# Where the SBUF tiles of a two-layer backbone kernel begin, modulo 512 bytes

## The chip, the core and the metric

The kernel runs on one core of a Trainium2 chip. The metric is the device time of one execution in microseconds (us). SBUF is the on-chip memory that the engines read. A tile of 128 partitions begins at the same byte in each partition, and this text calls that byte modulo 512 the tile's **place**. TensorE is PE in the profile, and PEld is its weight load. VectorE is DVE, ScalarE is ACT, GpSimd is POOL, and SyncE (SP) issues the DMAs.

## What is computed

A layer of the first kind (a gated depthwise convolution of 31 taps beside windowed attention) is followed by one of the second kind (a gated convolution of 3 taps), and by a final RMS norm. Tokens: 512, with a context of 256; width 1024, inner width 2048. Most of the arithmetic is in four matrix products:

```python
h = xn @ w_in                                  # layer one: 1024 -> 4608 columns
x = x + gt * ((concat(a, att) * silu(gate)) @ ev_w_out)
h = xn @ od_w_in                               # layer two: 1024 -> 8192 columns: bg, cg, u, z
x = x + gt * ((bg * conv3(cg * u) * silu(z)) @ od_w_out)
return rms_norm(x, final_g)
```

## The kernel before

Both operands of a product are split in two halves of type float32r, a rounded `h` and the rest `l`, and each product is three matmuls:

```python
def mm3(out, wh, wl, xh, xl, start, stop):
    T.matmul(out, lhsT=wh, rhs=xh, start=start, stop=False)
    T.matmul(out, lhsT=wh, rhs=xl, start=False, stop=False)
    T.matmul(out, lhsT=wl, rhs=xh, start=False, stop=stop)
```

The tile given as `lhsT` is stationary: a LDWEIGHTS loads 128 columns of it (512 bytes of each partition) ahead of its matmul. The tile given as `rhs` is moving: the matmul streams it, 512 columns (2048 bytes) in most. Each matmul has a LDWEIGHTS of its own, also where the stationary tile is the one before.

`proj` makes a projection: 8 steps over the width of 1024, so 24 matmuls into one PSUM bank, with the weight tile stationary and the activations moving. Layer two runs `mixer(j)` for j = 0 to 15, and each calls `in_proj(j)`: four projections (`pcg`, `pu`, `pbg`, `pz`), 96 matmuls. For j = 0 they are cut into halves of 256 columns. For j = 1 to 15 they are whole: 15 x 96 = 1440 matmuls of 512 columns. After that the outputs `f` are made, in two halves of the model's width, with the weights `wf` moving and the activations `z1h`, `z1l` stationary; a weight block `wf_0` to `wf_7` holds two of the 16 steps. In layer one, the projections `pq`, `pk`, `ag`, `av`, `pg` are mixed among the matmuls of attention (`s`, `pt`, `po`), `pgc` comes after them, and then come 8 projections `pya` with weights `woa` (192 matmuls) on the gated attention.

All operations are recorded and put into an order by a planner that uses costs written in the code; it knows nothing of addresses. So each operation is issued from one line, L481. SBUF comes from one pool. A tile has a tag, and the pool gives a tag one block of buffers when the tag is first used; block follows on block in that order. Tags of small or odd size (`cols` with 1664 bytes, columns of 4 to 128 bytes) are first used between the large ones, so the large ones begin at different places. In the built program they are:

| tag | holds, where TensorE reads it | place before | place after |
|---|---|---|---|
| `wh`, `wl` | weight halves: stationary in projections, moving in `f` | 256 | 128 |
| `xn` | activations of layer one (moving); `z` of the convolution; `z1` for j < 8 (stationary in `f`) | 256 | 128 |
| `q` | queries (stationary in `s`); `z1` for j = 8 to 11 | 256 | 128 |
| `D` | keys; first weights `ws`; gated attention `z8` to `z15` (moving in `pya`); `yh`, `yl` (moving in layer two); last three `wf` blocks of the second half | 384 | 128 |
| `p` | attention weights; weights of `in_proj(0)`; `z1` for j = 15 | 384 | 128 |
| `vv` | values (stationary in `po`); weights of `in_proj(0)` | 384 | 128 |
| `th`, `tl` | transposed attention weights (moving in `po`); `z1` for j = 12 and 13 | 128 | 128 |
| `tmp`, `sg`, `wsv`, `rx`, `pacc`, `wr` | work tiles; `sg` holds `z1` for j = 14 | 256, 256, 256, 128, 0, 320 | 128 |
| `A`, `B`, `rope`, `ad` | tokens, `x1`, modulation weights | 384 or 128 | the same |
| `ident`, `ones` | identity of the transposes, row of ones | 320, 256 | the same |

Slices of a tile that TensorE takes begin 512 or 1024 bytes further on, so they have the tile's place.

Of the kernel before, what the change touches and what calls it, by code (L numbers as in the profile page):

```python
# [11 lines left out]
F32 = mybir.dt.float32  # L12
# [7 lines left out]
P = 128  # L20
D = 1024
# [463 lines left out]
def backbone_kernel(ctx, tc, x_d, ctx_d, xT_d, c_d, cT_d, cols_d, ada0_d, ada1_d, adas_d, ws_d, wi0_d, woa_d, woc_d, wi1_d, wo1_d,  # L485
# [11 lines left out]
    pool = ctx.enter_context(tc.tile_pool(name="sb", bufs=1))  # L497
    ps = ctx.enter_context(tc.tile_pool(name="ps", bufs=1, space=PSUM))

    def new(shape, dt, tag, name, bufs, space=pool):  # L500
        t = LTile(space, shape, dt, tag, name, bufs, space is ps)
        return View(t, [], 0, shape[0], t.ix, dt)


    phases = Phases(lambda k: tc.tile_pool(name=f"ps{k}", bufs=1, space=PSUM))
# [5 lines left out]
    def bank(tag, name):  # L511
        if tag == "c":
            return phased(2, (P, 512), "c", name, 3)
        return new((P, 512), F32, tag, name, {"b": 4, "cv": 1}[tag], ps)
# [3 lines left out]
    def unit(tag, name, dt=F32, shape=(P, 512)):  # L518
        return new(tuple(shape), dt, tag, name, TAGS[tag])


    dm = new((P, 1), F32, "dm", "dm", 1)
    V.memset(dm, 1.0)
    A_.activation(dm, dm, AF.Silu)
# [329 lines left out]
    vv = new((P, NB, NKV, P), F32R, "vv", "vv", 1)  # L854
# [199 lines left out]
    with plan.after(turned[-1]), plan.stream("ada", ADA_BIAS):  # L1054
        silc = new((P, D), F32, "rope", "silc", 1)
        SP.dma_start(out=silc, in_=c_d[0:1, :].to_broadcast([P, D]))
        for n in range(2):
            th = unit("tmp", f"silt{n}")
# [369 lines left out]
```

## Time and profile before

| | us |
|---|---|
| median of 3 runs (lowest, highest) | 1018.12 (1016.85, 1019.17) |
| the profiled execution: its own time | 1019.33 |
| its span, first to last instruction | 1017.5 |
| PE busy in the span | 982.0 |
| DVE, ACT, POOL busy in the span | 609.6, 488.5, 412.5 |

Matmuls overlap each other, so the length that the profile gives for one (0.39 us or so for 512 columns) is not what it costs. In a stretch without gaps the cost of one is the distance from its start to the next one's start: the starts of the first and the last row of a run of matmuls, divided by their number. The text calls this the spacing.

### The profile page before, as it was taken

The numbers are of one execution on the slowest core, as the hardware profiler recorded it, in microseconds if no ns is written. First come the engines' busy times: TensorE is split into PE (matmuls) and PEld (weight loads), VectorE is DVE, ScalarE is ACT, GpSimd is POOL, SyncE is SP. The second block draws the span as 40 slices with busy tenths as digits, with TensorE's granted clock in tenths as the row PEclk, the third lists the DMA queues.
The fourth block names the chain that finished last, engine by engine and source line by source line (L and its number), as shares of the span: only waits on it lengthen the run. The fifth ranks groups of instructions, "written<-read, shape, count | busy, mean of one in ns | idle before, by whom it ended". The sixth has DMA issues, their size and how long they took to land.

```text
span 1017.5 us, 13484 instructions
## 1 busy us (share of the span) xinstructions
PE 982.0 (97%) x4996; PEld 806.0 (79%) x4996; DVE 609.6 (60%) x982; ACT 488.5 (48%) x923; POOL 412.5 (41%) x368
## 2 busy tenths in 40 slices
PE   8989999999999997799998999999999999999997
PEld 5888777778787786588898988888888888888886
DVE  4735878978888888856217576444444444542343
ACT  6637779676797754344326332232223223222232
POOL 5616887666979867878867000000000000000011
PEclk9989999999999999799999999999999999999999
DMA  8632111012122335243254245223222322322322
GB/s 323 228 120 82 65 43 39 26 61 95 51 84 105 118 108 188 81 168 104 82 173 140 83 156 175 104 83 104 84 102 83 104 96 92 104 83 84 102 83 83
DMA packets 31750, 109.11 MB, mean 107 GB/s; under 512 B 3650, under 2 KB 3778, under 8 KB 31684
## 3 DMA queue, kind: packets, MB, share of 16 engines
q1 hardware_dynamic: 31684, 108.25, 31.0%
q8 instruction: 39, 0.64, 0.3%
q14 instruction: 27, 0.22, 0.1%
HBM read 106.14 MB, written 2.10 MB: 106 GB/s over the span
## 4 chain that ended last, share of the span: by engine, by line
PE 76%; DVE 9%; DMA 5%; ACT 4%; POOL 3%; issue 2%; SPq 0%; POOLq 0%; DVEq 0%; ACTq 0%
PE pbg L481 9%; PE pz L481 9%; PE pcg L481 9%; PE pu L481 9%; PE f L481 8%; PE pya L481 5%; PE s L481 3%; DVE cv L481 3%; PE po L481 3%; PE pt L481 3%; PE ag L481 3%; PE pq L481 3%; PE av L481 3%; PE pg L481 2%; PE pgc L481 2%
## 5 line engine op out<-in xcount | busy, mean ns | idle before, releaser
L481 POOL TENSOR_TENSOR x1t<-x1t,fg 128x512 f32<-128x512 f32 x4 | 6.8, 1738 | 402.1 <-ACT fy L481 402.1
L481 DVE SCALAR_TENSOR_TENSOR cv<-u,cols,cv 128x512 f32<-128x512 f32 x180 | 135.5, 753 | 12.2 <-ACT cv L481 8.2
L481 POOL TENSOR_TENSOR cp<-cp,pr 128x512 f32<-128x512 f32 x60 | 78.9, 1315 | 3.5 <-ACT pr L481 1.6
L481 DVE TENSOR_TENSOR tl<-pt,th 128x512 fp32r<-128x512 f32 x72 | 48.1, 689 | 22.6 <-ACT th L481 21.4
L481 PE MATMUL pt<-ident,p 128*128 128x128 f32 x288 | 49.5, 277 | 3.4 <-ACT p L481 2.8
L481 ACT ACTIVATE th<-pt 128x512 fp32r<-128x512 f32 x72 | 41.1, 595 | 20.3 <-PE pt L481 19.4
L481 ACT ACTIVATE p<-s,nm 128x512 f32<-128x512 f32 (+1 forms) x64 | 46.9, 739 | 7.3 <-DVE nm L481 6.9
L481 PEld LDWEIGHTS pt<-ident,p 128*128 128x128 f32 x288 | 35.8, 140 | 17.2 <-ACT p L481 10.1
L481 DVE TENSOR_REDUCE s<-s 128x2 f32<-128x1024 f32 (+1 forms) x32 | 43.5, 1360 | 4.1 <-PE s L481 3.7
L481 ACT ACTIVATE pr<-u,cols 128x512 f32<-128x512 f32 x60 | 41.4, 718 | 5.6 <-POOL cp L481 4.1
L481 PE MATMUL po<-th,vv 128*128 128x512 f32 x72 | 31.2, 433 | 0.6 <-ACT th L481 0.5
L481 PE MATMUL po<-tl,vv 128*128 128x512 f32 x72 | 31.0, 431 | 0.2 <-DVE tl L481 0.2
L481 DVE TENSOR_TENSOR ya<-ya,sz 128x512 f32<-128x512 f32 x16 | 11.1, 691 | 32.4 <-ACT sz L481 32.3
L481 DVE SCALAR_TENSOR_TENSOR ac<-ac,silc 128x1024 f32<-128x1024 f32 x6 | 9.6, 1599 | 31.9 <-DMA ac<-in_ada_dram 31.9
L481 ACT ACTIVATE sz<-pz 128x512 f32<-128x512 f32 x16 | 9.6, 597 | 36.0 <-PE pz L481 36.0
L481 DVE SCALAR_TENSOR_TENSOR ya<-cu,cols,ya 128x512 f32<-128x512 f32 x32 | 24.1, 752 | 1.1
L481 PEld LDWEIGHTS pmod<-ccol,adas 128*128 128x128 f32 x128 | 19.0, 226 | 2.8 <-DMA adas<-in_adas_dram 2.2
L481 DVE TENSOR_TENSOR ya<-pbg,ya 128x512 f32<-128x512 f32 x16 | 11.1, 692 | 14.5 <-PE pbg L481 14.4
L481 PE MATMUL pmod<-ccol,adas 128*128 128x2 f32 x128 | 18.7, 267 | 0.9 <-DMA adas<-in_adas_dram 0.6
L481 ACT ACTIVATE tp<-tp,mab 128x512 f32<-128x512 f32 (+1 forms) x16 | 10.2, 640 | 19.1 <-PE tp L481 13.5
L481 PEld LDWEIGHTS po<-th,vv 128*128 128x128 f32 x72 | 13.5, 188 | 6.6 <-ACT th L481 5.7
L481 PEld LDWEIGHTS po<-tl,vv 128*128 128x128 f32 x72 | 13.7, 190 | 5.1 <-DVE tl L481 3.3
(1671 smaller groups left out, 3460.7 us busy)
## 6 DMA issues: line engine op xcount, KB each, us to landing
wicg<-in_wi_dram SPq DMA_DIRECT2D x16, 512.0 KB, 3.3
wiu<-in_wi_dram SPq DMA_DIRECT2D x16, 512.0 KB, 3.3
wibg<-in_wi_dram SPq DMA_DIRECT2D x16, 512.0 KB, 3.3
wiz<-in_wi_dram SPq DMA_DIRECT2D x16, 512.0 KB, 3.4
wf<-in_wo_dram SPq DMA_DIRECT2D x16, 512.0 KB, 3.3
adas<-in_adas_dram SPq DMA_DIRECT2D x8, 512.0 KB, 4.0
ada<-in_ada_dram SPq DMA_DIRECT2D x8, 512.0 KB, 5.0
wb<-in_wi_dram SPq DMA_DIRECT2D x8, 512.0 KB, 3.4
```

Source lines behind the costliest of these rows:

```text
L481: op.a = op.fn(*a, **k)
```

## The change

Before any tile of the kernel is used, one tile of each of 15 tags is taken from the pool and not used. All 15 sizes are multiples of 512 bytes, so their blocks follow on each other at one place, and the tags of odd size come behind them. The row of instructions of each engine, and the semaphores that each instruction waits for, are the same as before; only addresses differ. The places that result are in the last column of the table above.

```diff
+    for tag, n, bufs in (("wr", 1024, 3), ("D", 512, 16), ("xn", 512, 16), ("q", 512, 8), ("wh", 512, 4), ("wl", 512, 4),
+                         ("tmp", 512, 4), ("p", 640, 8), ("vv", 3072, 1), ("th", 512, 2), ("tl", 512, 2), ("wsv", 256, 8),
+                         ("sg", 512, 2), ("rx", 512, 1), ("pacc", 512, 1)):
+        pool.tile([P, n], F32, tag=tag, name=f"place_{tag}", bufs=bufs)
+
+
     phases = Phases(lambda k: tc.tile_pool(name=f"ps{k}", bufs=1, space=PSUM))
```

## Rows read from the trace of the kernel before

**Rows 1.** The page: busy time, share of the span and instructions of each engine.

```profile
PE 982.0 (97%) x4996; PEld 806.0 (79%) x4996; DVE 609.6 (60%) x982; ACT 488.5 (48%) x923; POOL 412.5 (41%) x368
```

**Rows 2.** Busy time by stretch: attention, `pya`, layer two's projections, first half of `f`.

```profile
core 0: us, PE busy (x) PEld busy (x) DVE busy (x) ACT busy (x) POOL busy (x), PEclk, DMA share, GB/s
78.00:386.00 308.00, 303.15 (x1625) 238.91 (x1625) 252.06 (x387) 232.03 (x447) 231.37 (x208) 1.00 0.23 77
...
451.00:500.00 49.00, 48.57 (x224) 39.23 (x224) 26.93 (x39) 21.30 (x36) 40.20 (x31) 1.00 0.29 97
...
584.00:920.00 336.00, 336.00 (x1442) 270.27 (x1442) 164.02 (x271) 100.00 (x166) 0.00 (x0) 1.00 0.31 105
920.00:966.00 46.00, 46.00 (x210) 37.82 (x209) 15.56 (x23) 13.75 (x24) 1.81 (x2) 1.00 0.27 92
```

**Rows 3.** The chain that ended last, in order of time: start us, us, what.

```profile
584.10 5.60 PE pcg L481 x24
...
936.27 69.97 PE f L481 x334
```

**Rows 4.** Timeline of PE: first matmul of `in_proj(1)`, first of `f` (start us, us).

```profile
583.94 0.40 PE L481 MATMUL pcg<-yh,wicg1h 128*128 128x512 f32 x1
...
919.94 0.39 PE L481 MATMUL f<-wf_0h,z1h 128*128 128x512 f32 x1
```

**Rows 5.** Timeline of PE: projection `av` 5 of layer one, first, and the 24 behind.

```profile
233.78 0.39 PE L481 MATMUL av<-xh,wa5h 128*128 128x512 f32 x1
...
239.22 0.39 PE L481 MATMUL av<-xl,wa4h 128*128 128x512 f32 x1
```

**Rows 6.** Timeline of PE: first matmuls of `pya` 4 and of `pya` 5.

```profile
476.43 0.40 PE L481 MATMUL pya<-z8h,woa4h 128*128 128x512 f32 x1
...
482.03 0.40 PE L481 MATMUL pya<-z8h,woa5h 128*128 128x512 f32 x1
```

**Rows 7.** Timeline of PE, first half of `f`: first matmuls with `wf` 5, 6, 7.

```profile
949.30 0.39 PE L481 MATMUL f<-wf_5h,z1h 128*128 128x512 f32 x1
...
954.75 0.40 PE L481 MATMUL f<-wf_6h,z1h 128*128 128x512 f32 x1
...
960.34 0.39 PE L481 MATMUL f<-wf_7h,z1h 128*128 128x512 f32 x1
```

**Rows 8.** Timeline of PE, second half of `f`, third block of tokens.

```profile
1001.90 0.39 PE L481 MATMUL f<-wf_5h,z1h 128*128 128x512 f32 x1
...
1003.29 0.39 PE L481 MATMUL f<-wf_6h,z1h 128*128 128x512 f32 x1
...
1004.66 0.40 PE L481 MATMUL f<-wf_7h,z1h 128*128 128x512 f32 x1
...
1005.37 0.39 PE L481 MATMUL f<-wf_7h,z1h 128*128 128x512 f32 x1
...
1005.83 0.40 PE L481 MATMUL f<-wf_7h,z1l 128*128 128x512 f32 x1
```

**Rows 9.** Timeline of PE, second half of `f`: behind a run of 256 columns.

```profile
971.41 0.40 PE L481 MATMUL f<-wf_1h,z1h 128*128 128x512 f32 x1
...
972.80 0.39 PE L481 MATMUL f<-wf_1h,z1h 128*128 128x512 f32 x1
```

**Rows 10.** Timeline of PE: matmuls of 256 columns, `in_proj(0)` and `f`.

```profile
574.77 0.28 PE L481 MATMUL pbg<-yl,w 128*128 128x256 f32 x1
...
575.97 0.28 PE L481 MATMUL pu<-yh,wiu0l 128*128 128x256 f32 x1
...
1006.06 0.28 PE L481 MATMUL f<-wf_5h,z1h 128*128 128x256 f32 x1
...
1006.30 0.28 PE L481 MATMUL f<-wf_5h,z1l 128*128 128x256 f32 x1
```

**Rows 11.** Groups of DVE in 695.94 to 718.35 us: count, busy us, mean ns.

```profile
L481 DVE TENSOR_TENSOR wiz6l<-wiz,wiz6h 128x512 fp32r<-128x512 f32 x2 | 1.4, 694 | 4.2 <-ACT wiz6h L481 4.2
...
L481 DVE TENSOR_TENSOR z1l<-ya,z1h 128x512 fp32r<-128x512 f32 x1 | 0.7, 693 | 0.1
```

## The prediction

> **What bounds the kernel now.** I read the page first, then busy time by stretch, then the chain of waits, and last the timeline of PE row by row. The page shows PE busy for 982.0 of 1017.5 us [rows 1], and the stretches show where that is a bound [rows 2]: in layer two's projections PE is busy for all of 336.00 us, with DVE at 164.02, ACT at 100.00, POOL at nothing and the DMA engines at 0.31. In `pya` it is 48.57 of 49, in the first half of `f` 46.00 of 46. The chain that ended last goes through PE there without a break, projection after projection of 24 matmuls in 5.60 us, then 334 matmuls of `f` in 69.97 us [rows 3]. So from 584 us to about 1006 us only the spacing of the matmuls counts, and a shorter spacing shortens the kernel one to one. Attention is less pure: PE 303.15 of 308, DVE 252.06, ACT 232.03 [rows 2].
>
> **Two spacings.** The timeline is to be read for starts, not lengths. From the first matmul of `in_proj(1)` to the first of `f` there are 1440 matmuls of 512 columns in 919.94 - 583.94 = 336.00 us: 233.3 ns each [rows 4]. The projection `av` 5 has the same shape, the same code and the same count, and takes 239.22 - 233.78 = 5.44 us: 226.7 ns each [rows 5]. `pya` 4 takes 482.03 - 476.43 = 5.60 us: 233.3 ns [rows 6]. [...]
>
> What differs is the pair of places. `av` streams `xn` (256) over `wh`, `wl` (256). `pya` and layer two stream `D` (384) over the same tags (256). That alone could still be the stage, so I looked for a stage in which the pair changes and nothing else does. That is `f`, with `wf` moving and `z1` stationary:
> - first half, `wf` 5 over `q`: 256 and 256, 24 matmuls in 954.75 - 949.30 = 5.45 us, 227.1 ns [rows 7];
> - first half, `wf` 6 over `th`, `tl`: 256 and 128, 960.34 - 954.75 = 5.59 us, 232.9 ns [rows 7];
> - second half, `wf` 5 (now in `D`) over `q`: 384 and 256, 6 matmuls in 1003.29 - 1001.90 = 1.39 us, 231.7 ns [rows 8];
> - second half, `wf` 6 (in `D`) over `th`, `tl`: 384 and 128, 1004.66 - 1003.29 = 1.37 us with the odd pair at its end, 228 ns [rows 8].
>
> Each stationary tag and each moving tag stands once in a fast pair and once in a slow one. So it isn't the tag, the engine that wrote it, or the stage: where the two places differ by 0 or 256 the spacing is about 227 ns, where they differ by 128 it is about 233. I call the first pairs even and the second odd. An odd pair costs 233.3 - 226.7 = 6.6 ns more.
>
> **The change part by part.** No instruction and no wait is added, removed or moved, so the change costs nothing in itself. The 15 unused tiles take no time. What it does is to make every pair among the 15 tags even (128 and 128). Counted in the program's order of matmuls, of 512 columns each:
> - Layer two, j = 1 to 15: 1440 odd pairs become even: 1440 x 6.6 = 9.5 us [rows 4, 5]. All of it is on the chain [rows 3].
> - `pya`: 192 odd pairs (24 x 8) become even: (5.60 - 5.44) x 8 = 1.3 us [rows 5, 6]. On the path, PE is busy throughout there [rows 2].
> - `f`: 36 odd pairs in the first half and 27 in the second: 63 x 6 = 0.4 us [rows 7, 8].
> - Attention, 78 to 386 us: 170 matmuls of 512 columns go from odd to even, at most 170 x 6.6 = 1.1 us. Against that, 127 short matmuls (transposes by `ident`, which stays at 320, and the masks) are now followed by a stationary tile at 128 in place of 256, an odd difference. The trace has no clean run of such a pair. With nothing or 6.6 ns each as bounds the cost is 0 to 0.8 us. A gain on either side can also be lost in waits for ACT and DVE. I take 0.3 us of gain, bounds -0.8 and +1.1.
> - Matmuls of 256 columns: the pairs of `in_proj(0)` are even already (384 and 384), 10 in 1.20 us, 120 ns [rows 10]. An odd pair (`wf` 5 in `D` over `q`) takes 2 in 0.24 us, the same, so I take nothing for them [rows 10].
> - First 78 us: about 150 odd pairs become even, at most 150 x 6.6 = 1.0 us. Most are of 256 columns, and the weights are still being loaded there, so I take nothing.
> - DVE, ACT and POOL read and write at other places too. DVE's subtraction of two halves takes 694 ns with its tiles at 256, 320 and 256, and 693 ns with all three at 256 [rows 11]. I take nothing, for ACT and POOL too.
>
> Sum: 9.5 + 1.3 + 0.4 + 0.3 = 11.5 us. Against its own time the profiled execution would go from 1019.33 to 1007.8. It lies 1.2 us over the median of 1018.12, so as a median I expect **1006.6 us**, 0.989 of before.
>
> **The one price that isn't in the trace.** No pair of before is 128 and 128. The nearest rows are 384 and 128, and 256 and 256, both at 227 ns; they show that neither the 256 nor the difference of 256 matters. The other bound are the rows of 384 and 384 at the end of `f` (`wf` 7 over `p`): two matmuls in 1005.83 - 1005.37 = 0.46 us, 230 ns [rows 8]. I take 226.7, because those two stand between odd pairs, and even pairs need some matmuls to settle: behind a run of 256 columns, 6 even pairs of 256 and 256 take 972.80 - 971.41 = 1.39 us, 231.7 ns [rows 9], and then drop to 227. Layer two has no such disturbance between its 1440 matmuls.
>
> [...] The trace has 226.7 and 233.3 ns for the same matmul with its tiles at other places [rows 5, 6]. [...]
>
> **The rivals.**
> - *No change, 1018.1.* The two reads don't meet, and 6.6 ns is a property of the stage (what ACT and DVE do beside it, which banks are written). For it: most odd pairs lie in two stages. Against it: within `f`, the spacing changes at the very matmul at which the pair changes, in both directions [rows 7, 8].
> - *The place itself matters, 1010 to 1017.* If 128 and 128 settles between 227 and 230 ns as 384 and 384 may [rows 8], the 1690 odd pairs on the path (1440 + 192 + 63, less a few at seams) gain less and some 1185 pairs that are even already (attention, `pgc`, `f`) lose. At 228.5: 1690 x 4.8 - 1185 x 1.8 = 6.0 us of gain, 1012.1. At 230: 1.7 us, 1016.4.
> - *Slower, 1026.* Two reads that begin at one place might always meet. If 128 and 128 costs what an odd pair costs, 233.3 ns, layer two and `pya` gain nothing and the 1185 even pairs lose 6.6 ns each: 7.8 us more, 1025.9. The change turns slower where the spacing of 128 and 128 passes 230.6 ns, since 1690 x (233.3 - s) = 1185 x (s - 226.7) there. Against it: 256 and 256 is also one place, and it is the fastest pair that the trace has [rows 5, 7].
> - *Another bound takes over.* In 336 us DVE works for 164.02 and ACT for 100.00 [rows 2], and 9.5 us less leaves both far off. I give it no chance of its own.
>
> **How the numbers follow.** The forecast (10 to 13 us of gain, so 1005 to 1008.5) has 0.80, a greater gain by way of attention 0.02, the place itself 0.08, no change 0.05, slower 0.05. The runs of before spread over 0.23%, so 0.2% (2 us) is about what can be told from no change. Faster by more than that: 0.80 + 0.02 + 0.06 of the third = 0.88. Within it: 0.02 + 0.05 = 0.07. Slower: 0.05. The range takes in the bounds of attention and the nearer part of the third case: 1004.5 to 1011.
>
> **What would show it.** In the profile after: projections of layer two with 24 matmuls in 5.44 us instead of 5.60, the first matmul of `f` some 11 us earlier and 326.4 us behind the first of `in_proj(1)`; `pya` in 5.44; `av` unchanged at 5.44; `wf` 5, 6 and 7 all alike in `f`; the same durations on DVE, ACT and POOL. I am wrong if `av` and `pgc` rise above 5.44 (then the place itself matters), or if layer two keeps 5.60 (then the pair was never the cause).

## The result, and the profile after

| | us |
|---|---|
| change: median of 4 runs (lowest, highest) | 1003.82 (1001.84, 1005.3) |
| before, beside it: median of 4 runs (lowest, highest) | 1017.49 (1013.75, 1019.17) |
| ratio, 95% interval | 0.9869 [0.9836, 0.9902] |
| profiled execution of the change: time, span | 1005.3, 1003.5 |

The change is faster, as forecast. Its median lies 2.8 us under the forecast of 1006.6 and 0.7 us under the lower end of the range. The page after stands against [rows 1]: PE has 12.0 us less, the number of its instructions is the same, and DVE (3.8) and POOL (3.2) have less too.

```profile
PE 970.0 (97%) x4996; PEld 806.4 (80%) x4996; DVE 605.8 (60%) x982; ACT 487.7 (49%) x923; POOL 409.3 (41%) x368
```

The timeline of PE after, with the two rows that answer to [rows 4]. The 1440 matmuls of layer two now take 906.37 - 579.94 = 326.43 us, 226.7 ns each, where it was 336.00 and 233.3.

```profile
579.94 0.40 PE L481 MATMUL pcg<-yh,wicg1h 128*128 128x512 f32 x1
...
906.37 0.39 PE L481 MATMUL f<-wf_0h,z1h 128*128 128x512 f32 x1
```

The same view for `av` 5 (the first and the 24 behind, as [rows 5]), `pya` 4 and 5 (as [rows 6]), and `f` with `wf` 5, 6 and 7 (as [rows 7]). `av` keeps 5.44 us, `pya` goes from 5.60 to 5.44, and `wf` 5 and 6 take 5.44 each, where it was 5.45 and 5.59.

```profile
235.69 0.39 PE L481 MATMUL av<-xh,wa5h 128*128 128x512 f32 x1
...
241.13 0.39 PE L481 MATMUL av<-xl,wa4h 128*128 128x512 f32 x1
...
474.34 0.39 PE L481 MATMUL pya<-z8h,woa4h 128*128 128x512 f32 x1
...
479.78 0.39 PE L481 MATMUL pya<-z8h,woa5h 128*128 128x512 f32 x1
...
935.72 0.39 PE L481 MATMUL f<-wf_5h,z1h 128*128 128x512 f32 x1
...
941.16 0.39 PE L481 MATMUL f<-wf_6h,z1h 128*128 128x512 f32 x1
...
946.60 0.39 PE L481 MATMUL f<-wf_7h,z1h 128*128 128x512 f32 x1
```

**Where the rest came from.** Each kernel was profiled three times in all (before: the first profile, `e0_before`, `e9_before_again`; the change: the first, `e1_after`, `e10_after_again`). The table has the distance between the starts of the first matmuls of stages on the timeline, in us. `lnm` are two matmuls that begin the norm behind `pgc`, and the first of them counts here; `pyb` are the projections behind `pya`.

| stage | forecast gain | before, three profiles | change, three profiles | gain of the means |
|---|---|---|---|---|
| start to first `ag` | 0 | 80.1, 81.3, 82.3 | 82.3, 78.3, 82.3 | 0.3 |
| attention, to first `pgc` | 0.3 | 307.1, 306.9, 307.1 | 306.8, 306.9, 306.8 | 0.2 |
| first `pgc` to `lnm` | 0 | 20.1, 20.0, 19.7 | 18.0, 17.3, 18.0 | 2.1 |
| `lnm` to `pya` 1 | 0.2 | 52.4, 52.2, 51.4 | 50.9, 50.4, 51.1 | 1.2 |
| `pya` 1 to `pyb` 2 | 1.1 | 40.62, 40.62, 40.62 | 39.49, 39.49, 39.49 | 1.1 |
| `pyb` 2 to `in_proj(1)` | 0 | 83.7, 83.6, 86.3 | 82.4, 83.0, 82.6 | 1.9 |
| layer two, j = 1 to 15 | 9.5 | 336.00, 336.00, 336.00 | 326.43, 326.42, 326.43 | 9.6 |
| `f`, to the end | 0.4 | 97.6, 97.6, 97.6 | 97.1, 97.1, 97.1 | 0.5 |

Of the stages with a forecast all but `lnm` to `pya` 1 came out within 0.2 us. Of those without one, the first varies by 4 us within one kernel, so its 0.3 says nothing. The other two, 387 to 408 us and 500 to 584 us, gave 4.0 us that the prediction doesn't have, and `lnm` to `pya` 1 gave 1.0 more than its share: 5.0 us together. The three profiled executions of before (1019.33, 1020.14 and 1022.82 us) are longer than the median of 25 timed runs (1015.63), so these sums stand for the profiles, and the timed runs show less.

**A held instruction.** Around 395 us DVE has one instruction of 128x1024, `as<-as,silc`; its tiles are of the tags `ad` and `rope`, whose places the change leaves. Before, it takes 5.51 us, where the three others of its form in the same profile take 1.23 to 1.45, and ends about 1 us behind the last of a row of POOL subtractions. The timelines of DVE and of POOL before:

```profile
394.31 5.51 DVE L481 SCALAR_TENSOR_TENSOR as<-as,silc 128x1024 f32<-128x1024 f32 x1
...
393.61 1.32 POOL L481 TENSOR_TENSOR z15l<-att,z15h 128x512 fp32r<-128x512 f32 x1
394.85 2.62 POOL L481 TENSOR_TENSOR wgc2l<-wgc,wgc2h 128x512 fp32r<-128x512 f32 x2
397.38 1.37 POOL L481 TENSOR_TENSOR wgc3l<-wgc,wgc3h 128x512 fp32r<-128x512 f32 x1
```

After, it takes 1.60 us, and it is POOL that stands back: its two `wgc2l` take 3.55 us, not 2.62.

```profile
395.78 1.60 DVE L481 SCALAR_TENSOR_TENSOR as<-as,silc 128x1024 f32<-128x1024 f32 x1
...
394.98 1.31 POOL L481 TENSOR_TENSOR z15l<-att,z15h 128x512 fp32r<-128x512 f32 x1
396.23 3.55 POOL L481 TENSOR_TENSOR wgc2l<-wgc,wgc2h 128x512 fp32r<-128x512 f32 x2
399.73 1.30 POOL L481 TENSOR_TENSOR wgc3l<-wgc,wgc3h 128x512 fp32r<-128x512 f32 x1
```

I call this the hold. The rows read as if one of the two engines waits for the other here: before, 5.51 us on DVE and 2.62 on POOL's two `wgc2l`, after, 1.60 and 3.55. What would make one wait for the other, no run shows. The next load into the single buffer of `as` waits for this instruction, then POOL's next `as`, `lnsum`, and PE's `lnm`. The timeline's first `pgc` and two rows of the chain of waits, before:

```profile
387.20 0.48 PE L481 MATMUL pgc<-xh,wgc0h 128*128 128x512 f32 x1
...
399.86 3.65 DMA as<-in_ada_dram
...
407.27 2.07 PE lnm L481 x2
```

and after:

```profile
389.11 0.48 PE L481 MATMUL pgc<-xh,wgc0h 128*128 128x512 f32 x1
...
397.42 5.99 DMA as<-in_ada_dram
...
407.15 1.12 PE lnm L481 x2
```

Without the hold the instruction is 3.9 us shorter, but the load behind it takes 5.99 us, not 3.65, and gives 2.3 us of that back. The instruction also starts 0.4 us earlier behind the first `pgc`. So `lnm` comes about 2 us earlier and not 4. In the waits of PE the row for `lnm` is, before and after (us in total, times, longest):

```profile
PE lnm L481 <- POOL lnsum L481: 5.5, 1, 5.5
```

```profile
PE lnm L481 <- POOL lnsum L481: 3.5, 1, 3.5
```

**The clock.** Between 400 and 570 us PE waits now and then, and the granted clock drops to 0.50 of full speed for a while: in steps of 2 us it stands there in 408 to 412, 428 to 432 and 554 to 556 us before, and in 410 to 412, 426 to 432 and 556 to 558 us after. Busy time by stretch before, columns as in [rows 2] (PEclk is the third number from the end):

```profile
404.00:416.00 12.00, 8.73 (x24) 5.60 (x25) 7.14 (x11) 5.69 (x10) 11.21 (x7) 0.72 0.29 100
424.00:436.00 12.00, 6.05 (x19) 4.86 (x20) 11.15 (x15) 1.75 (x4) 10.99 (x9) 0.72 0.26 88
500.00:508.00 8.00, 8.00 (x56) 7.71 (x55) 1.02 (x2) 3.12 (x5) 8.00 (x7) 0.79 0.33 100
550.00:566.00 16.00, 13.18 (x80) 12.53 (x81) 11.59 (x28) 11.53 (x27) 11.26 (x14) 0.79 0.29 100
```

and after:

```profile
404.00:416.00 12.00, 8.85 (x30) 6.47 (x31) 7.65 (x10) 6.08 (x11) 12.00 (x8) 0.86 0.38 114
422.00:436.00 14.00, 7.38 (x25) 5.95 (x25) 13.12 (x17) 3.36 (x7) 12.66 (x10) 0.76 0.22 75
500.00:508.00 8.00, 8.00 (x69) 8.00 (x69) 2.40 (x2) 3.47 (x6) 8.00 (x7) 1.00 0.56 167
550.00:562.00 12.00, 9.74 (x65) 9.03 (x64) 8.59 (x21) 8.20 (x19) 7.39 (x10) 0.86 0.26 88
```

A stretch times what its clock lacks is clock time lost: 12 x 0.28 + 12 x 0.28 + 8 x 0.21 + 16 x 0.21 = 11.8 us before, 12 x 0.14 + 14 x 0.24 + 0 + 12 x 0.14 = 6.7 us after. Part of it is lost while PE waits anyway. Summed in the same way over steps of 2 us from 380 to 600 us, the three profiles of before lose 12.0, 10.3 and 11.9 us and those of the change 6.8, 8.5 and 6.8.

### The profile page after: what moved, and what is told of

The parts are those of the page before. It is cut to its first block, busy times and chain, and to the rows that moved or that the text cites. A ratio compares the mean times of both kernels' runs of the same rounds, so it can differ in the third digit from the quotient of the medians.

```text
span 1003.5 us, 13484 instructions
## 1 busy us (share of the span) xinstructions
PE 970.0 (97%) x4996; PEld 806.4 (80%) x4996; DVE 605.8 (60%) x982; ACT 487.7 (49%) x923; POOL 409.3 (41%) x368
## 4 chain that ended last, share of the span: by engine, by line
PE 77%; DVE 7%; POOL 4%; DMA 4%; ACT 4%; issue 2%; SPq 0%; POOLq 0%; ACTq 0%; DVEq 0%
PE pbg L481 9%; PE pcg L481 9%; PE pz L481 9%; PE pu L481 9%; PE f L481 8%; PE pya L481 6%; PE pq L481 3%; DVE cv L481 3%; PE s L481 3%; PE po L481 3%; PE ag L481 3%; PE pt L481 3%; PE av L481 2%; PE pgc L481 2%; PE sv L481 2%
## 5 line engine op out<-in xcount | busy, mean ns | idle before, releaser
L481 DVE TENSOR_TENSOR tl<-pt,th 128x512 fp32r<-128x512 f32 x72 | 48.1, 689 | 22.6 <-ACT th L481 21.1
L481 PEld LDWEIGHTS pt<-ident,p 128*128 128x128 f32 x288 | 35.7, 140 | 17.1 <-ACT p L481 9.9
```

The source lines that it names most:

```text
L481: op.a = op.fn(*a, **k)
```

## The experiments

All builds have the instructions of the kernel before; only places differ. The loop of the change got a table of places, and a filler tile ahead of each tag whose place differs. Each experiment below is one such table; "before" stands for the places of before (`wr` 320; `wh`, `wl`, `xn`, `q`, `tmp`, `sg`, `wsv` 256; `p`, `vv`, `D` 384; `pacc` 0).

```diff
+    PLACE = {...}
+    at = 128
     for tag, n, bufs in (("wr", 1024, 3), ("D", 512, 16), ..., ("pacc", 512, 1), ("", 0, 0)):
+        place = PLACE.get(tag, 128)
+        if place != at:
+            pool.tile([P, (place - at) % 512 // 4], F32, tag=f"pad_{tag}", name=f"pad_{tag}", bufs=1)
+        if tag:
             pool.tile([P, n], F32, tag=tag, name=f"place_{tag}", bufs=bufs)
+        at = place
```

**1. `e0_before`, `e1_after`: both kernels as they are.**

> The kernel before once more, unchanged. Two theories of the gain beyond the forecast of 11.5 us: (V) it is variation of the waits around the layer norm (386 to 452 us) and in the first 50 us, where PE waits for POOL, DVE and DMA; then the wait for lnsum, 5.5 us in the first profile of before and 3.5 in that of the change, comes out anywhere between 3 and 6 us here, and the time is within 3 us of 1017.5. (S) the places shorten those waits; then lnsum is again 5.5 +- 0.3 us here. Both: 24 matmuls of layer two in 5.60 us, of av 5 in 5.44.

> The changed kernel once more, unchanged. Both theories: 24 matmuls of layer two in 5.44 us, of pya in 5.44. (V): the wait for lnsum is anywhere between 3 and 6 us, the ratio to before over five rounds is 0.988 to 0.990 (a gain of 10.5 to 12.5 us). (S): the wait is again 3.5 +- 0.3 us and the ratio is 0.985 to 0.988.

Measured: before 1014.84 us (10 runs, 1009.89 to 1020.14), ratio to the runs of before beside it (median 1015.63, 25 runs, 1009.01 to 1021.26) 0.9994 [0.9965, 1.0023]. The change 1003.72 (6 runs), 0.9893 [0.9858, 0.9929]. Runs of one kernel spread over 12 us, much more than the three runs shown ahead of the prediction (1016.85 to 1019.17), which lay on the upper side. The wait for `lnsum` is 5.5 us in `e0_before`, as (S) has it; in `e1_after` it is 2.8, below both, and the ratio of 0.9893 lies in the range of (V), not in that of (S). So the timed runs don't show the whole gain of the profiles.

**2. `e2_only_D`: of all tags only `D` is moved.**

```diff
-    PLACE = {before, "D": 384}
+    PLACE = {before, "D": 256}
```

> All places as before, but tag D (yh, yl, z8 to z15, keys) at 256 instead of 384, so that it is even with wh and wl at 256. Pair theory (only the difference of moving and stationary tile modulo 256 counts): layer two and pya go from 5.60 to 5.44 us per 24 matmuls, a gain of 9.5 + 1.3 us; f stays mixed; ratio 0.988 to 0.990, nearly all of the whole change. Rival (TensorE needs all of its tiles at one place, or the place 128 itself is the fast one): layer two stays at 5.60 and the ratio is 0.998 to 1.002, since xn, q, wh stay at 256, p and vv at 384, th at 128.

Measured: 1005.99 us (8 runs), 0.9909 [0.9878, 0.994]. A row of the chain of waits (start, us, what) in layer two shows 24 matmuls with `D` at 256 over `wh`, `wl` at 256:

```profile
588.94 5.44 PE pu L481 x24
```

One tag of fifteen brings most of the gain; the ratio lies a little above the 0.988 to 0.990 expected. The hold is still there (5.54 us).

**3. `e3_w_odd`: the change, but the weight halves 128 away.**

```diff
+    PLACE = {"wh": 256, "wl": 256}
```

> All places as in the change (128), but wh and wl at 256. Pair theory: every projection pair becomes odd; av 5, ag 1 and pgc 1 go from 5.44 to 5.60 us per 24, layer two and pya stand at 5.60 again, f with wf moving is odd but for its last blocks in D; time 1017 to 1021, as before or up to 3 us above it (f and pgc lose 2 us more than they did before). Rival (the place of the moving tile alone counts: 384 is slow, 128 and 256 are fast): moving tiles stand at 128 in projections, so 5.44 everywhere and 1004 us.

Measured: 1018.69 us (10 runs), 1.0025 [0.9993, 1.0058]. Now all projections are slow, those of layer one too: `av` 5 takes 239.00 - 233.40 = 5.60 us. The timeline of PE:

```profile
233.40 0.40 PE L481 MATMUL av<-xh,wa5h 128*128 128x512 f32 x1
...
239.00 0.40 PE L481 MATMUL av<-xl,wa4h 128*128 128x512 f32 x1
```

and the chain of waits:

```profile
583.71 5.60 PE pu L481 x24
```

So fast pairs can be made slow by moving only the weights: it is neither the stage nor what stands beside it, nor the place of the moving tile alone.

**4. `s1_sweep`, `s2_sweep`, `s3_sweep`: other differences.**

```diff
+    PLACE = {"D": 192, "xn": 160, "q": 224, "th": 192, "tl": 192}     # s1: layer one 32, layer two 64
+    PLACE = {"D": 320, "xn": 224, "q": 160, "th": 288, "tl": 288}     # s2: layer one 96, layer two 192
+    PLACE = {"D": 32}, all others 288                                 # s3: layer one 0, layer two 256
```

> Places as in the change, but xn at 160, D at 192, q at 224, th and tl at 192, so that pairs differ (moving minus stationary, modulo 256) by 32 in layer one, 64 in layer two and pya, and in f by 224 (wf 0 to 3), 160 (wf 4, 5) and 192 (wf 6). Three theories of how the cost goes with the difference d. Proportion: it grows from 0 at d = 0 to 6.6 ns at 128 and falls again: 228.3 ns at 32 (24 in 5.48 us), 230.0 at 64 (5.52), 228.3 at 224, 231.7 at 160, 230.0 at 192. Step: every d but 0 costs all of it: 233.3 everywhere (5.60). Bit: only the bit of 128 counts: 226.7 at 32 and 64 (5.44), 233.3 at 160, 192 and 224. If a difference gives less than 226.7 ns, none of the three is complete.

> Places as in the change, but xn at 224, D at 320, q at 160, th and tl at 288: the pairs differ by 96 in layer one, 192 in layer two and pya, and in f by 160 (wf 0 to 3), 224 (wf 4, 5) and 96 (wf 6). Proportion: 231.7 ns at 96 (24 in 5.56 us), 230.0 at 192 (5.52), 231.7 at 160, 228.3 at 224. Step: 233.3 everywhere (5.60). Bit: 226.7 at 96 (5.44), 233.3 at 192, 160 and 224.

> All 15 tags at place 288, but D at 32: layer one's projections pair 288 with 288 (a difference of 0 at a place that no run has had), layer two and pya pair 32 with 288 (a difference of 256 over a long run, which before only had in 24 matmuls of f). Theory 'difference': 24 matmuls take 5.44 us in all three. Rival 'only equal places': 5.44 in layer one, 5.60 in pya and layer two, time 1015 or more. Rival 'place itself': layer one away from 5.44 as well.

Measured, one run each: 1002.21, 1020.26 and 999.48 us. For each, `av` 5 on the timeline of PE and then a row of layer two in the chain of waits. First s1:

```profile
230.23 0.40 PE L481 MATMUL av<-xh,wa5h 128*128 128x512 f32 x1
...
235.83 0.40 PE L481 MATMUL av<-xl,wa4h 128*128 128x512 f32 x1
```

```profile
577.68 5.49 PE pu L481 x24
```

then s2:

```profile
236.13 0.39 PE L481 MATMUL av<-xh,wa5h 128*128 128x512 f32 x1
...
241.73 0.39 PE L481 MATMUL av<-xl,wa4h 128*128 128x512 f32 x1
```

```profile
589.32 5.60 PE pu L481 x24
```

and s3:

```profile
232.96 0.39 PE L481 MATMUL av<-xh,wa5h 128*128 128x512 f32 x1
...
238.40 0.39 PE L481 MATMUL av<-xl,wa4h 128*128 128x512 f32 x1
```

```profile
579.74 5.44 PE pu L481 x24
```

Place of the moving tile less that of the stationary one, and the spacing:

| difference | 0 | 32 | 64 | 96 | 128 | 192 | 256 |
|---|---|---|---|---|---|---|---|
| 24 matmuls, us | 5.44 | 5.60 | 5.49 | 5.60 | 5.60 | 5.60 | 5.44 |
| spacing, ns | 226.7 | 233.3 | 228.9 | 233.3 | 233.3 | 233.3 | 226.7 |

Here the difference decides, and not in proportion: 32 costs as much as 128 (5.60 us). None of the three theories holds whole: "step" fails at 64 alone, "proportion" at 32, 96 and 192, "bit" at 32, 64 and 96. The sign counts too: 64 takes 5.49 us, 192 (64 the other way) 5.60. In `f` of s1 and s2, 160 and 224 take 5.59 to 5.63 us for 24. Places that are equal at 128, 256 and 288 are alike (5.44 us each), so among these the place itself doesn't matter.

**5. `e4_only_wr`, `e5_wr_320`, `e6_wr_192`, `e7_wr_256`: what makes the hold?** The raw weight blocks lie in `wr`, and POOL subtracts the rounded half (`wh`) from them; before, the two lie 64 bytes apart.

```diff
+    PLACE = {before, "D": 384, "wr": 128}     # e4
+    PLACE = {"wr": 320}                       # e5
+    PLACE = {"wr": 192}                       # e6
+    PLACE = {before, "D": 384, "wr": 256}     # e7
```

> All places as before, but tag wr (the raw weights, which ACT and POOL or DVE read to split them) at 128 instead of 320. In the three profiles with before's wr one DVE multiplication of as is held for 5.5 us behind a row of POOL subtractions, and in the three with wr at 128 it takes 1.6. (W) the place of wr decides which of the two gets its turn: here the DVE as takes 1.6 us, the distance from the first pgc to lnm falls from 21.1 us to 17.7 to 18.6, and the ratio is 0.996 to 0.999. (V) it is chance, or hangs on other tags: 5.5 us, 21.1 us and a ratio of 0.999 to 1.001. Both: layer two at 5.60 us per 24.

> All places as in the change, but wr back at 320. (W): the DVE as is held for 5.5 us again, first pgc to lnm 21.1 us, and the time lies 2 to 3 us above that of the change: ratio 0.990 to 0.993. (V): 1.6 us and 17.7 to 18.6 us as in the change, ratio 0.987 to 0.990. Both: layer two and pya at 5.44 us per 24, since TensorE reads wr only in the first microseconds.

> The change with wr moved to 192, so that a raw weight block (wr) and its rounded half (wh, at 128) lie 64 bytes apart again, as before (320 and 256). Question: what holds VectorE's 128x1024 instruction as<-as,silc behind GpSimd's row of subtractions. Theory 'pair wr-wh': the hold is back, that instruction takes 5.5 us instead of 1.6, first pgc to first lnm 21.1 us instead of 17.9 to 18.6, GpSimd's subtraction 1306 ns instead of 1292, and the time is 2.5 to 3 us longer than with the change, ratio to before 0.990 to 0.992. Theory 'hazard of the moment' (how the instructions happen to meet decides, the places only by way of that): not held, 1.3 to 1.9 us, ratio 0.985 to 0.989. On both, 24 matmuls take 5.44 us in layer one and two.

> The kernel before with wr moved from 320 to 256 alone: raw block and rounded half begin at the same place, everything else as before. Theory 'pair wr-wh': not held, as<-as,silc 1.3 to 1.9 us, first pgc to first lnm 17.7 to 18.6 us, subtraction 1292 ns; ratio to before 0.997 to 0.999. Theory 'hazard of the moment': either. On both, layer two keeps 5.60 us for 24 matmuls and layer one 5.44.

Measured: e4 1015.26 us (12 runs), 0.9981 [0.9962, 0.9999]; e5 1001.95 (6 runs), 0.9848 [0.9818, 0.9878]; e6 1001.93 (4 runs), 0.9868 [0.9814, 0.9923]; e7 1015.05 (10 runs), 0.9997 [0.9968, 1.0027]. None of the four is held: `as<-as,silc` takes 1.85, 1.32, 1.35 and 1.61 us. So `wr` at 320 alone isn't the cause (e5), nor 64 bytes between `wr` and `wh` (e6). The ratios settle less: e4's interval ends just below 1, e7 lies above the 0.997 to 0.999 that its theory of no hold gave, and e5 below the ranges of both theories. Those 64 bytes do show in POOL's subtraction itself. Groups of POOL (count, busy us, mean ns), e6 and then e5:

```profile
L481 POOL TENSOR_TENSOR wg_0l<-wg,wg_0h 128x512 fp32r<-128x512 f32 x8 | 10.4, 1304 | 12.3 <-ACT wg_0h L481 12.3
```

```profile
L481 POOL TENSOR_TENSOR wg_0l<-wg,wg_0h 128x512 fp32r<-128x512 f32 x8 | 10.4, 1295 | 12.3 <-ACT wg_0h L481 12.3
```

That group takes 1304 to 1308 ns in the builds with the two 64 bytes apart, and 1291 to 1297 ns in all others.

**6. `e8_wr320_w256`, `e9_before_again`, `e10_after_again`: build or execution?**

```diff
+    PLACE = {"wr": 320, "wh": 256, "wl": 256, "D": 256, "xn": 256, "q": 256}     # e8
```

> The change with wr at 320 and wh, wl, D, xn, q at 256, so that the weight blocks and their halves lie where they lay before, and every long pair that TensorE reads still differs by 0. Theory 'these two places': VectorE's as<-as,silc is held for 5.5 us behind GpSimd's row, first pgc to first lnm 21.1 us, though layer two runs at 5.44 us. Theory 'hazard of the execution' (held in some executions whatever the places): no forecast for one look, about 3 in 13.

> The kernel before, profiled once more. If the hold belongs to the build: 5.5 us a third time, and 21.1 us from first pgc to first lnm. If it is a matter of the execution: it may take 1.3 to 1.9 us here, and 17.7 to 18.9 us.

> The changed kernel, profiled once more. If the hold belongs to the build: not held, 1.3 to 1.9 us. If it is a matter of the execution: it may be held, 5.5 us, with 21 us from first pgc to first lnm.

Measured, one run each: 1004.22, 1022.82 and 1005.66 us. The timelines of DVE of e8, of before and of the change:

```profile
391.74 5.49 DVE L481 SCALAR_TENSOR_TENSOR as<-as,silc 128x1024 f32<-128x1024 f32 x1
```

```profile
396.25 5.49 DVE L481 SCALAR_TENSOR_TENSOR as<-as,silc 128x1024 f32<-128x1024 f32 x1
```

```profile
395.95 1.62 DVE L481 SCALAR_TENSOR_TENSOR as<-as,silc 128x1024 f32<-128x1024 f32 x1
```

The hold belongs to the build. In 16 profiles it stands in the five with `wr` at 320 and `wh`, `wl` at 256 (before three times, e2, e8: 5.49 to 5.54 us) and in none of the other eleven (1.32 to 1.85 us). With it, `lnm` starts 19.4 to 20.1 us behind the first `pgc`, without it 17.1 to 18.4 us. (The expectations' 21.1 and 17.7 to 18.9 us run to the second of its two matmuls.) The load of `as` behind it takes 3.6 us in the five and 5.0 to 6.0 in the eleven. In e8 layer two runs at 5.44 us all the same: the hold and the spacing are two things. Which of the moved tags makes the hold together with `wr` isn't separated: `xn` and `q` stood at 256 in all five too. Nor does the moment alone decide: DVE's instruction starts 0.69 to 0.71 us behind POOL's `z15l` in the five, 0.52 to 1.06 in the eleven.

The 16 profiles also tell what each is worth from the first `pgc` to `in_proj(1)`. Where 24 matmuls of `pya` take 5.6 us (5.57 to 5.60), that distance is 196.5 to 198.0 us with the hold (before) and 190.8 to 193.6 without (e3, e4, e7, s2). Where they take 5.44, it is 193.2 and 194.0 with the hold (e8, e2) and 187.7 to 191.2 without (the change, e5, e6, s3). So in these profiles the hold goes with about 4 us and the odd pair with about 3, where the forecast has 1.3 for `pya`.

## Why the prediction was right in its mechanism and short in its sum

- *The pair of places sets the spacing:* right, shown in both directions (experiments 2 and 3). "No change" and "the place itself matters" fall, the latter by three equal places at 226.7 ns. "Slower" falls with them: equal places gave 226.7 ns, and no difference that was tried gave less. It isn't the clock either: the granted clock is 1.00 in the 336.00 us of before [rows 2] and in the 326.43 us of the change. What in TensorE or SBUF makes the difference, no run shows; the reads that meet or don't meet, of which the rivals speak, were a supposition.
- *Odd and even:* too narrow. I called differences of 0 and 256 even and of 128 odd, since before had no others. For this change that does no harm, but differences of 32 (s1) and 192 (s2) took as much as 128 did: 5.60 us for 24.
- *Layer two 9.5, `pya` 1.3, `f` 0.4, attention 0.3:* 9.6, about 1.3, 0.5 and 0.2. The pair of 128 and 128 needed no price of its own.
- *256 columns and the first 78 us, nothing:* no profile speaks against it, but the first stage varies by 6 us over all profiles (76.3 to 82.3), so it could not be seen.
- *The step that failed:* "DVE's subtraction ... I take nothing, for ACT and POOL too." I asked whether an instruction's own duration depends on its places and took the answer of one DVE form for three engines. POOL's subtraction is 11 to 17 ns shorter, which is nothing by itself. But one DVE instruction was held for 5.5 us behind POOL by the places of before, and by those of the change it takes 1.6. `lnm` comes 2.1 us earlier, since the load of `as` gives 2.3 of the 3.9 back. The row was there to be seen: an instruction of 5.51 us whose form takes 1.23 to 1.45 elsewhere, on the path to `lnm`. I read PE only. The sign "the same durations on DVE, ACT and POOL" didn't come true.
- *How much of it reaches the end:* in the profiles, 5.0 us more than forecast between 387 and 584 us, with 4.0 us less clock time lost (means of 11.4 and 7.4). In the timed runs less. e4 and e7 are before without the hold, and they gain 0.2% and nothing sure. e2, which is held, lies 2.3 us above the change beside it, with intervals that overlap. The change's two ratios, 0.9869 and 0.9893, both hold the forecast's 1006.6 / 1018.12 = 0.9887 in their intervals, so the timed runs alone don't show a gain beyond the sum.
- *The level:* the forecast was counted from 1018.12. Before had medians of 1017.49 and 1015.63 later. 0.9887 of these is 1006.0 and 1004.2. So in the first comparison 0.6 of the 2.8 us that the forecast was too high is level, and the rest would be gain beyond the sum; in `e1_after` (1003.72) 2.4 of 2.9 us is level.
- *The lower end of the range:* too near. "The runs of before spread over 0.23%, so 0.2% (2 us) is about what can be told" was read from three runs; later runs of before reach from 1009.01 to 1021.26, 1.2%. The lower end, 1004.5, has no term for that, and the 0.7 us by which the median lies under it is smaller than the shift of before's own median (1018.12 to 1015.63). (10 us of gain is also 1008.1 and not 1008.5.)

What stays open: why just 320 and 256 lead to the hold, that is, why POOL goes on from one subtraction to the next there; why the load of `as` takes longer without the hold (two loads of `x` are issued 4.9 us ahead of it before and 1.1 us ahead of it after, but no run moves them alone); and the 1.9 us between `pyb` 2 and `in_proj(1)`. There the clock fell once more in two of the three profiles of before (0.79 in 500 to 508 us) and not in `e0_before`, so the execution has a part in it. That fall isn't the hold's: e3 and e7 have it without the hold, e2 and e8 don't have it with the hold. All four profiles that have it take 5.60 us for 24 matmuls of `pya`, and none of those at 5.44 has it. That the shorter wait for `lnm` is the reason for the higher clock behind it is argued from rows that stand side by side; it wasn't tried alone. No build beat the change by more than its interval; e5 and e6 stand beside it.

## What to carry to other kernels

Where a stage is bound by matmuls that follow without a gap, look at the start addresses of its moving and its stationary tile: here, for matmuls of 512 columns in float32r with a LDWEIGHTS each, among the differences tried only places that are equal modulo 256 bytes gave 226.7 ns (228.9 at 64, 233.3 at 32, 96, 128 and 192), and moving one tag (`D`) was worth 0.9%. Judge it by the spacing of starts in a run without gaps, not by the length of a matmul (0.39 or 0.40 us here at both spacings). And where addresses move, look for single instructions that take several times what their form takes elsewhere: here one took 5.51 us where others of its form took 1.23 to 1.45, and with other places it took 1.60. What such an instruction loses isn't what the kernel loses: follow what waits for it to the end.

## What was not expected of the hardware

- In this kernel a matmul of 512 columns in float32r took 226.7 ns where its two operands begin 0 or 256 bytes apart (modulo 512), 228.9 ns at 64, and 233.3 ns at 32, 96, 128 and 192.
- The DVE instruction `as<-as,silc` took 5.49 to 5.54 us in five profiles of five with `wr` at 320 and `wh`, `wl` at 256, and 1.32 to 1.85 us in eleven others. In the first profile of before it ended 1.1 us behind three POOL subtractions that all began after it, and POOL's two `wgc2l` took 2.62 us; in the first of the change they took 3.55.
- The load that waits for that instruction took 3.6 us behind the hold and 5.0 to 6.0 us without it.
- POOL's 128x512 subtraction `wg_0l` took 1304 to 1308 ns with its inputs 64 bytes apart and 1291 to 1297 ns otherwise.
